# Retention and attention kernel: token sums, decay tables, chunk ends and a gate modulation in other places

## Chip, core and metric

The kernel runs on one core of a Trainium2 chip. The metric is the device time of one execution in microseconds (us). The engines are TensorE (PE, with its weight loads as PEld), VectorE (DVE), ScalarE (ACT), GpSimd (POOL) and SyncE (SP, which here only issues DMAs). DMAs are issued from the queues of SP, ACT and POOL.

## What is computed

Two layers over 256 latent tokens and 256 context tokens of width 2048, batch 1, all in float32. Each layer normalises its input, modulates it by a shift and a scale that come from a condition vector `c` (adaLN), runs a token mixer, multiplies the mixer's result by a SiLU gate of the input, projects it, and adds it back under a gate `gt` that also comes from `c`.

```python
for i in range(DEPTH):                                  # 2 layers
    mod_l = c_act @ ada_w[i] + ada_b[i]                 # shift, scale, gate: 3 x 2048 each
    mod_c = cc_act @ ada_w[i] + ada_b[i]
    sh_l, sc_l, gt_l = jnp.split(mod_l, 3, axis=-1)
    ...
    h_l = _rms_norm(x, norm_gain[i]) * (1 + sc_l[:, None]) + sh_l[:, None]
    h_c = _rms_norm(ctx, norm_gain[i]) * (1 + sc_c) + sh_c
    y_l, y_c = mixer(h_l, h_c, ...)   # layer 0: retention, 8 heads; layer 1: windowed attention, 16 heads
    x = x + gt_l[:, None] * y_l
    if i < DEPTH - 1:
        ctx = ctx + gt_c * y_c
```

The retention mixer scores queries against keys with powers of a decay per head and direction; its scores are multiplied by tables of such powers. The second layer's context result is not needed, so of its gate only the latent tokens' half is computed: the part (1, 2) of the modulation.

## The kernel before

**Products.** Weights stream through SBUF in tiles `wraw` of 512 KB (five buffers, loaded on SP's queue). A float32 product is made of three matmuls, so each tile is split: ACT casts its high half `wh` (L143), DVE subtracts to get the low half `wl` (L114); each has three buffers. TensorE then runs high × high, low × high and high × low (L151 to L153) into PSUM: five accumulators `acc` and three smaller `pm`. A chunk of 512 output columns needs eight such weight tiles.

**Layer 0.** First come the query-key chunks of the first heads, then the value projection of all heads, then a loop over eight heads. In heads 0 to 3 the loop runs one chunk of eight tiles, the head's gate; in heads 4 to 7 a query-key chunk and then the gate chunk. Behind every weight tile a `hook` is called, and it puts in a piece of other work: the previous head's outputs in five tasks (`o0`, `o1`, `norm`, `l0`, `l1`), this head's decay tables (`dc`), scores (`sc`), the values' load and split (`v`, `vs`), and a number of modulation steps. Which task stands behind which tile is written out in lists (`plan`, `begin`). A scheduler then orders each engine's instructions.

**Clearing a chunk.** `evac` rotates the four accumulators of a query-key chunk (rope) and splits them: `t` and `sw` (L975 to L977) and `r_h`, `r_l`. The next chunk's matmuls need those accumulators.

**Modulation steps.** The modulation by `c` is not a matmul: a tile of `adaB` (512 KB, SP's queue) is multiplied by a row of `c` (`crow`) and summed in one DVE instruction (L690), with a short read of the sum behind it. There are 224, all in layer 0: two for each of 96 tiles (latent and context tokens), and one for each of 32 tiles of the part (1, 2).

**Token sums.** The output projection of layer 0 is done with seven products in place of eight (as Strassen's), so it needs sums and differences of the two token blocks of the gated heads, `a` to `d`. `parts` makes five of them per head, M1, M3, M4, M6 and M7, on POOL (L1058, tile `ue`, two buffers), and stores each to DRAM `uB_d` on POOL's queue (L1062); `a` and `d` themselves go out on ACT's queue. For the last head M1 and M4 are made on DVE and stay in SBUF. The projection, right behind, loads the sums back and splits them; its result `x` (L1217, L1218) lies in the memory that the last head's sums leave.

**Decay powers.** At the end of the first chunks the decay powers, transposed in `gT`, go to DRAM (`gamT_d`, `pow_d`), and one DMA of 1024 rows of 1020 bytes copies them skewed into `skew_d` (L656). All of these stand on ACT's queue. The heads read their tables `dd` from `skew_d`.

**Layer 1.** K and V projections, then four query chunks (q0 to q3) and four gate chunks (g0 to g3) in turn; behind each weight tile `pump` puts in two pieces of the attention. The last part is the second output projection.

Of the kernel before, what the change touches and what calls it, by code (L numbers as in the profile page):

```python
# [15 lines left out]
ALU = mybir.AluOpType  # L16
# [6 lines left out]
T = 512  # L23
# [29 lines left out]
def backbone(ctx: ExitStack, tc, xT_d, w0_d, wo0_d, w1_d, wo1_d, adaS_d, adaB_d,  # L53
# [340 lines left out]
    with tc.tile_pool(name="pa", bufs=1) as pa:  # L394
# [218 lines left out]
        for u in range(2, 9):  # L613
# [31 lines left out]
            if u == 7:  # L645

                gp = m_tile()
                with after():
                    pe[0] = nc.tensor.transpose(gp[0:64, 0:P], gam.rearrange("p a b -> p (a b)"), ident).ins
                gT = pb.tile([P, P], F32, name="gT", tag="dd")  # L650
                nc.scalar.copy(gT[0:64], gp[0:64, 0:P])
                nc.scalar.dma_start(out=gamT_d.rearrange("d k h t -> (d k h) t"), in_=gT[0:64])
                nc.scalar.dma_start(out=pow_d[:, 0:127], in_=gT[40:48, 1:P])
                nc.scalar.dma_start(out=pow_d[:, 127:128], in_=ones[0:H, 0:1])
                nc.scalar.dma_start(out=pow_d[:, 128:255], in_=gT[0:H, 0:127])
                nc.scalar.dma_start(out=skew_d.rearrange("h (r x) -> h r x", x=255),  # L656
                                    in_=pow_d.unsqueeze(1).to_broadcast([H, P, 255]))
# [18 lines left out]
    def ada_parts(parts, ntk):  # L676
        for layer, kind in parts:
            part = 3 * layer + kind - 2
            asum = const.tile([P, 2, KB, ntk], F32, name="asum", tag=f"asum{ntk}")
            for q in range(2):  # L680
                if q not in rows_at:
                    rows_at.clear()
                    rows_at[q] = [crow(adap[0], f"crow{t}", t, q) for t in range(2)]
                    yield "row"
# [16 lines left out]
    jobs = chain(ada_parts(((0, 2), (1, 0), (1, 1)), 2), ada_parts(((1, 2),), 1))  # L701
# [10 lines left out]
    with tc.tile_pool(name="ph", bufs=1) as ph:  # L712
# [130 lines left out]
        def hook():  # L843
            count[0] += 1
            n = count[0]
            if n > 4:
                with tc.issue_after(last_lo[0]), tc.issue_after(last_hi[0]):
                    next(stats, None)
            if n <= 4 or n % 2:
                ada_step(2 + (n <= 4))  # L850
            next(sums, None)

# [89 lines left out]
    if True:  # L942
# [108 lines left out]
        def parts(h, u, to=None):  # L1051

            a, b, c, d = (u[k][:, :, L * t:L * t + L] for k in range(2) for t in range(2))
            for m, x, y, op in ((M4, a, c, ALU.subtract), (M1, a, d, ALU.add), (M6, a, b, ALU.add),
                                (M7, c, d, ALU.add), (M3, b, d, ALU.subtract)):
                ue = pb.tile([P, 2, L], F32, name="ue", tag="ue", bufs=2)
                now = to is not None and m in (M1, M4)
                (nc.vector if now else nc.gpsimd).tensor_tensor(out=ue, in0=x, in1=y, op=op)  # L1058
                if now:
# [3 lines left out]
            for m, x in ((M2, a), (M5, d)):  # L1063
                nc.scalar.dma_start(out=uB_d[m, h], in_=x)
# [7 lines left out]
        def output_tasks(h, sg, gated=True):  # L1072
# [10 lines left out]
            def last(f):  # L1083
# [4 lines left out]
                if f and gated:  # L1088
                    parts(h, sg)
# [19 lines left out]
        def begin(plan, ada):  # L1109
            state["plan"], state["ada"] = iter(plan), iter(ada)  # L1110
# [18 lines left out]
        for h in range(H):  # L1129
# [3 lines left out]
            if h < 4:  # L1133
                e = [lambda g=qkr, i=i, h=h: evac(h, g, (i, 2 + i)) for i in range(2)]
                if h:
                    o0, o1, norm, l0, l1 = outs
                    plan = [[o0], [o1, dc], [e[0], v], [e[1], norm], [sc[0]], [l0, sc[1]], [l1, vs, sc[2]], [sc[3]]]
# [4 lines left out]
                begin(plan, [2 * (h > 0 or n > 3) for n in range(8)])  # L1142
            else:
                o0, o1, norm, l0, l1 = outs
                begin([[o0], [o1], [dc], [norm, v], [], [l0], [l1, vs], []], [3, 3, 3, 3, 3, 3, 2, 1])
                accs = gemm_ws(w0_d, 3 * h, 8, h_mov, T, hook=hook)
# [3 lines left out]
                begin([[], [], [], [sc[0]], [sc[1]], [sc[2]], [sc[3]], []], [2] * 8)  # L1150
# [5 lines left out]
        assert not list(jobs)  # L1156
# [3 lines left out]
                outs[1:2] + [(M4, 0), (M4, 1)], outs[2:3] + [(M4, 5), (M4, 6), (M4, 2), (M4, 3)],  # L1160
# [12 lines left out]
        parts(H - 1, sg, {m: unit(m, H - 1) for m in (M1, M4)})  # L1173
# [238 lines left out]
    open_slots("r2z")  # L1412

    with tc.tile_pool(name="pe", bufs=1, side="right") as pe:
# [54 lines left out]
        accs = gemm_ts(w1_d, 1, 8, h1_stat, 4)  # L1469
# [3 lines left out]
        def gate(c):  # L1473
            accs = gemm_ws2(w1_d, 2 + c, 8, 0, hook=lambda: pump(PUMP))
# [6 lines left out]
        def queries(c):  # L1481
            accs = gemm_ts(w1_d, 6 + c, 8, h1_stat, 2, hook=lambda: pump(PUMP))
# [84 lines left out]

        for g in range(4):
            accs = gemm_ws2(wo1_d, g, 8, 1, pre=(lambda kp: pump(5 if kp < 6 else 100)) if g == 0 else None,
                            tail=1 if g < 3 else 2)  # L1570
            for j in range(4):
# [18 lines left out]
                nc.scalar.dma_start(out=out_d[kb], in_=xb)  # L1590
    close_top()
# [102 lines left out]
```

## Time and profile before

| | before |
|---|---|
| median of three runs, us | 1962.4 |
| lowest and highest, us | 1961.68, 1967.97 |
| profiled execution, us | 1965.91 |
| its span, first to last instruction, us | 1964.1 |
| mean granted TensorE clock | 0.995 |
| moved by DMA | 472.95 MB, mean 241 GB/s |

How to read the quoted lines: a line of a timeline gives the start in us, the duration in us, the engine (with q for its queue of DMA issues), the line of the kernel, the operation, output <- input, how many, and in brackets the idle time before it and what ended that. A line of the waits gives engine, what waited, `<-` what ended the wait, the total in us, how many times, the longest. A line of a tile gives min/median/max of one instruction in ns, and the first and last start. A line of the windows gives the stretch, its length, then for PE, PEld, DVE, ACT and POOL the busy us and (x count), the granted clock, the DMA engines' share and GB/s.

### The profile page before, as it was taken

How to read it: one execution, taken by the hardware profiler on the slowest of the kernel's cores; microseconds unless marked ns; L12 is line 12 of the kernel's file. 1: busy time of each engine (PE TensorE's matmuls, PEld its weight loads, DVE VectorE, ACT ScalarE, POOL GpSimd, SP SyncE). 2: the span in 40 equal slices, each digit the busy share in tenths (PEclk: the TensorE clock that was granted, in tenths of full speed). 3: DMA queues.
4: the chain of work that ended last, by engine and by line, in shares of the span. 5: the costliest groups of instructions: out<-in, count | busy, mean ns of one | idle time of the engine just before them, and what ended most of it. 6: DMA issues, size and time to landing. Idle time of an engine off the chain costs nothing.

```text
span 1964.1 us, 26030 instructions
## 1 busy us (share of the span) xinstructions
PE 1917.0 (98%) x9420; PEld 1578.6 (80%) x9420; DVE 1493.0 (76%) x2250; ACT 817.8 (42%) x1218; POOL 401.0 (20%) x446
## 2 busy tenths in 40 slices
PE   8999999999999999999999999899999999999999
PEld 4677878788787788878788778788888888888887
DVE  5577877877868998888888776677879746777764
ACT  4233434334444333222322235355555434766653
POOL 1201222222211444423323231200000000000000
PEclk9999999999999999999999999999999999999999
DMA  9969989989897877888989985579976325444464
GB/s 392 416 251 284 281 243 274 279 269 292 261 288 215 257 225 220 269 249 250 275 258 291 327 265 194 189 257 303 316 261 218 104 95 161 143 137 139 130 204 149
DMA packets 138842, 472.95 MB, mean 241 GB/s; under 512 B 17528, under 2 KB 33368, under 8 KB 133080
## 3 DMA queue, kind: packets, MB, share of 16 engines
q1 hardware_dynamic: 105792, 367.40, 54.3%
q0 software_dynamic: 15200, 49.30, 12.7%
q10 hardware_dynamic: 17720, 54.59, 7.9%
q8 instruction: 74, 1.21, 0.3%
q14 instruction: 56, 0.46, 0.1%
HBM read 440.22 MB, written 99.14 MB: 275 GB/s over the span
## 4 chain that ended last, share of the span: by engine, by line
PE 73%; DVE 12%; DMA 9%; issue 3%; ACT 2%; POOL 1%; ACTq 0%; SPq 0%; DVEq 0%; POOLq 0%
PE acc L153 11%; PE acc L151 11%; PE acc L152 11%; PE acc L1212 9%; PE acc L202 6%; DMA wraw<-in_w 5%; PE acc L1209 4%; DVE wl L114 4%; PE pm L152 3%; PE pm L153 3%; PE pm L151 3%; PE acc L199 3%; PE acc L531 2%; DVE wraw L690 2%; DMA wraw<-in_adaB 2%
## 5 line engine op out<-in xcount | busy, mean ns | idle before, releaser
L114 DVE TENSOR_TENSOR wl<-wraw,wh 128x1024 fp32r<-128x1024 f32 x416 | 510.7, 1234 | 264.6 <-ACT wh L143 256.2
L143 ACT CAST wh<-wraw 128x1024 fp32r<-128x1024 f32 x415 | 433.8, 1051 | 636.4 <-DMA wraw<-in_w 258.2
L151 PE MATMUL acc<-hT_h,wh 128*128 128x512 f32 x928 | 365.4, 394 | 13.0 <-DVE t L975 7.6
L153 PE MATMUL acc<-hT_h,wl 128*128 128x512 f32 x928 | 362.7, 391 | 1.1 <-DVE wl L114 1.1
L152 PE MATMUL acc<-hl,wh 128*128 128x512 f32 x928 | 362.9, 391 | 0.0
L333 POOL COPY pin_t<-wl 128x1 f32<-128x1 f32 x128 | 95.2, 744 | 675.9 <-DVE wl L114 666.9
L151 PEld LDWEIGHTS acc<-hT_h,wh 128*128 128x128 f32 x928 | 175.0, 189 | 53.5 <-issue 10.8
L153 PEld LDWEIGHTS acc<-hT_h,wl 128*128 128x128 f32 x928 | 175.0, 189 | 39.0 <-DVE wl L114 2.0
L152 PEld LDWEIGHTS acc<-hl,wh 128*128 128x128 f32 x928 | 175.2, 189 | 34.7
L690 DVE SCALAR_TENSOR_TENSOR wraw<-wraw,crow 128x1024 f32<-128x1024 f32 x128 | 170.9, 1340 | 6.6 <-DMA wraw<-in_adaB 5.8
L690 DVE SCALAR_TENSOR_TENSOR ajunk<-wraw,crow 128x1024 bf16<-128x1024 f32 x96 | 121.9, 1270 | 6.7 <-DMA wraw<-in_adaB 6.6
L153 PE MATMUL acc<-wh,hl 128*128 128x512 f32 x320 | 125.0, 391 | 0.0
L252 POOL TENSOR_TENSOR rs<-ms,mhalf 128x4 f32<-128x4 f32 (+1 forms) x23 | 28.4, 1236 | 418.2 <-DVE ms L246 306.9
L335 POOL DMA_DIRECT2D wS_d<-in_wo x128 | 101.0, 789 | 11.1 <-issue 8.8
L143 ACT CAST wh<-vt 128x1024 fp32r<-128x1024 f32 x48 | 50.4, 1051 | 99.0 <-DVE vt L117 75.9
L1058 POOL TENSOR_TENSOR ue<-sg 128x512 f32<-128x512 f32 x38 | 71.7, 1893 | 92.7 <-DVE sg L1048 46.5
L114 DVE TENSOR_TENSOR wl<-vt,wh 128x1024 fp32r<-128x1024 f32 x48 | 58.8, 1225 | 38.2 <-ACT wh L143 37.6
L152 PE MATMUL pm<-r_l,r_h 128*128 128x512 f32 (+1 forms) x216 | 75.1, 348 | 5.3 <-DVE r_l L114 5.3
L151 PE MATMUL pm<-r_h 128*128 128x512 f32 (+1 forms) x216 | 75.4, 349 | 3.1 <-DVE sg L1040 2.0
L152 PE MATMUL acc<-wl,hT_h 128*128 128x512 f32 x192 | 75.2, 392 | 0.5 <-DVE wl L114 0.5
L151 PE MATMUL acc<-wh,hl 128*128 128x512 f32 x192 | 75.4, 393 | 0.0
L152 PE MATMUL acc<-wl,hl 128*128 128x512 f32 x192 | 74.9, 390 | 0.0
(315 smaller groups left out, 3695.4 us busy)
## 6 DMA issues: line engine op xcount, KB each, us to landing
wraw<-in_w SPq DMA_DIRECT2D x288, 512.0 KB, 4.9
wraw<-in_adaB SPq DMA_DIRECT2D x128, 512.0 KB, 5.2
wraw<-in_wo SPq DMA_DIRECT2D x80, 512.0 KB, 4.6
wS_d<-in_wo ACTq DMA_DIRECT2D x128, 256.0 KB, 5.3
wS_d<-in_wo POOLq DMA_DIRECT2D x128, 256.0 KB, 6.7
wraw<-wS_d SPq DMA_DIRECT2D x64, 512.0 KB, 5.3
araw<-in_adaS SPq DMA_DIRECT2D x28, 1024.0 KB, 13.1
wraw<-uB_d SPq DMA_DIRECT2D x20, 512.0 KB, 5.5
```

The costliest lines, as they stand in the source:

```text
L114: return nc.vector.tensor_tensor(out=out, in0=a, in1=hi.bitcast(F32), op=ALU.subtract)
L143: last_hi[0] = nc.scalar.copy(wh, raw).ins
L151: nc.tensor.matmul(ps, lhsT=ah, rhs=bh, start=start, stop=False, skip_group_check=skip)
L152: nc.tensor.matmul(ps, lhsT=ah, rhs=bl, start=False, stop=False, skip_group_check=skip)
L153: return nc.tensor.matmul(ps, lhsT=al, rhs=bh, start=False, stop=stop, skip_group_check=skip).ins
L202: nc.tensor.matmul(accs[j], lhsT=wk, rhs=h1(kb, s).rearrange("p a t -> p (a t)"), start=(kb == 0), stop=False)
L333: pin = nc.gpsimd.tensor_copy(pin_t, last_wl[0][:, 0, 0:1].bitcast(F32)).ins
L335: nc.gpsimd.dma_start(out=wS_d[i, r, q, x], in_=wo0_d[(*SUMS[i][1], r, q, x)], accum_op=ALU.add, max_dma_last_dim=4096)
L690: nc.vector.scalar_tensor_tensor(out=junk, in0=flat, scalar=1.0, in1=rows_at[q][t], op0=ALU.mult, op1=ALU.mult, accum_out=asum[:, q, kb, t ...
L1058: (nc.vector if now else nc.gpsimd).tensor_tensor(out=ue, in0=x, in1=y, op=op)
L1209: last_pe[0] = nc.tensor.matmul(accs[j][:, 0:L], lhsT=wk, rhs=b[:, 0:L], start=False, stop=(kq == 3 and k == 3)).ins
L1212: nc.tensor.matmul(accs[j], lhsT=wk, rhs=b, start=(kq == 0 and k == 0), stop=False)
```

## The change

Four parts, which the diff below shows cut to its core.

1. The 32 modulation steps of part (1, 2) leave layer 0 and come in layer 1: one behind each weight tile of the value chunk (`hook1(True)`), then one behind every second tile of the query and gate chunks. Two more loads of `crow` go with them. The numbers of steps per tile in layer 0 are written anew: 4 fewer in each of heads 0 to 3 and in each of heads 4 to 6, 6 fewer in head 7.
2. All token sums are made on DVE. M6 comes with task `l0`, the others with `l1`; M7 and M3 are made in place in the gated head's own tile `sg` and stored from there, M6, M4 and M1 in `ue`. The stores stay on POOL's queue. The tasks of heads 1 to 3 move by up to a tile.
3. Query-key chunks of heads 4 to 7 run their last two weight tiles block by block (`tail=2`): each accumulator takes both tiles before the next begins. The hook that this would skip is called.
4. `gT` and the decay powers are stored on POOL's queue, and the skewed copy is cut into one DMA per head.

```diff
@@ gemm_ws
             elif kp < nkp - 1:
+                if hook is not None:
+                    hook()
                 continue
...
@@ decay powers
-                nc.scalar.dma_start(out=gamT_d.rearrange("d k h t -> (d k h) t"), in_=gT[0:64])
...
-                nc.scalar.dma_start(out=skew_d.rearrange("h (r x) -> h r x", x=255),
-                                    in_=pow_d.unsqueeze(1).to_broadcast([H, P, 255]))
+                nc.gpsimd.dma_start(out=gamT_d.rearrange("d k h t -> (d k h) t"), in_=gT[0:64])
...
@@ hook of the first chunks
+            if n % 2 == 0:
+                i = n // 2 - 1
+                nc.gpsimd.dma_start(out=skew_d[i].rearrange("(r x) -> r x", x=255),
+                                    in_=pow_d[i].unsqueeze(0).to_broadcast([P, 255]))
...
-    jobs = chain(ada_parts(((0, 2), (1, 0), (1, 1)), 2), ada_parts(((1, 2),), 1))
+    jobs = ada_parts(((0, 2), (1, 0), (1, 1)), 2)
...
+        def parts(h, u, k, to=None):
+            a, b, c, d = (u[k2][:, :, L * t:L * t + L] for k2 in range(2) for t in range(2))
+            def made(m, x, y, op):
+                ue = pb.tile([P, 2, L], F32, name="ue", tag="ue", bufs=2)
+                comb(ue, x, y, op)
+                if to is not None and m in to:
+                    split(to[m][:, :, 0:L], to[m][:, :, L:T], ue)
+                else:
+                    nc.gpsimd.dma_start(out=uB_d[m, h], in_=ue)
+            if k == 0:
+                made(M6, a, b, ALU.add)
+                nc.scalar.dma_start(out=uB_d[M2, h], in_=a)
+                return
+            made(M4, a, c, ALU.subtract)
+            made(M1, a, d, ALU.add)
+            for m, x, op in ((M7, c, ALU.add), (M3, b, ALU.subtract)):
+                comb(x, x, d, op)
+                nc.gpsimd.dma_start(out=uB_d[m, h], in_=x)
+            nc.scalar.dma_start(out=uB_d[M5, h], in_=d)
...
@@ heads 1 to 3, then heads 4 to 7
-                    plan = [[o0], [o1, dc], [e[0], v], [e[1], norm], [sc[0]], [l0, sc[1]], [l1, vs, sc[2]], [sc[3]]]
+                    plan = [[o0], [o1, dc, e[0]], [e[1]], [norm, v], [sc[0]], [l0, sc[1]], [vs, sc[2]], [l1, sc[3]]]
...
-                begin([[o0], [o1], [dc], [norm, v], [], [l0], [l1, vs], []], [3, 3, 3, 3, 3, 3, 2, 1])
-                accs = gemm_ws(w0_d, 3 * h, 8, h_mov, T, hook=hook)
+                begin([[o0], [o1], [dc], [norm, v], [], [l0], [l1, vs], []], (4, 4, 1, 2, 2, 1, 1, 0))
+                accs = gemm_ws(w0_d, 3 * h, 8, h_mov, T, hook=hook, tail=2)
...
@@ layer 1
+    jobs = ada_parts(((1, 2),), 1)
+    n1 = [0]
+    def hook1(always=False):
+        pump(PUMP)
+        n1[0] += 1
+        if always or n1[0] % 2:
+            with tc.issue_after(last_lo[0]):
+                next(jobs, None)
...
-        accs = gemm_ts(w1_d, 1, 8, h1_stat, 4)
+        accs = gemm_ts(w1_d, 1, 8, h1_stat, 4, hook=lambda: hook1(True))
...
-            accs = gemm_ws2(w1_d, 2 + c, 8, 0, hook=lambda: pump(PUMP))
+            accs = gemm_ws2(w1_d, 2 + c, 8, 0, hook=hook1)
```

(`comb` is a tensor-tensor operation on DVE, L117, and was there before.) Three places show how instructions move.

The first is ACT's queue behind the first query-key chunk, where the accumulators are copied to `qk0e` and stored to `qk_d`. Before:

```order
L642 COPY qk0e<-acc 128x512 [waits PE_49]
L656 DMA skew_d<-pow_d 1024x1x255 [waits DMAHW4_49,DMAHW2_49]
L643 DMA qk_d<-qk0e 128x512 [waits Activation_49]
L642 COPY qk0e<-acc 128x512 [waits PE_49]
L642 COPY qk0e<-acc 128x512 [waits DVE_49,PE_49]
L643 DMA qk_d<-qk0e 128x512 [waits DMAHW3_49,Activation_49]
```

and POOL's queue at that point of the program after the change (`qk1e` is the second chunk, `pin_t` and `wS_d` belong to the copying of weights for the output projection):

```order
L654 DMA gamT_d<-gT 64x128 [waits Activation_49]
L655 DMA pow_d<-gT 8x127
L657 DMA pow_d<-gT 8x127
L854 DMA skew_d<-pow_d 128x255 [waits DMASW3_49,DMASW2_49,DMASW0_49]
L854 DMA skew_d<-pow_d 128x255 x4
L854 DMA skew_d<-pow_d 128x255 [waits DMASW1_49]
L854 DMA skew_d<-pow_d 128x255 x2
L662 DMA qk_d<-qk1e 128x512 [waits DMASW4_49,DVE_49]
L662 DMA qk_d<-qk1e 128x512 [waits DMASW5_49,DVE_49]
L335 COPY pin_t<-wl 128x1 [waits DVE_49]
```

The skewed copy has left ACT's queue; its eight pieces stand together on POOL's, ahead of the second chunk's stores, although the program issues them in eight different hooks.

The second place is DVE at the end of head 4's query-key chunk (`acc` its accumulators; `wl` low halves of weight tiles, before those of the next chunk's first two tiles, after that of the chunk's own last). Before:

```order
L1048 SCALAR_TENSOR_TENSOR sg<-sg,vec,pm 128x512 x4
L114 TENSOR_TENSOR wl<-wraw,wh 128x1024 x2
L114 TENSOR_TENSOR r_l<-acc,r_h 128x256 x2
L975 TENSOR_TENSOR t_6729<-acc,ropeR 128x256
L976 TENSOR_TENSOR sw<-sw,ropeR 128x256
L975 TENSOR_TENSOR t_6740<-acc,ropeR 128x256
L977 TENSOR_TENSOR t_6729<-t_6729,sw 128x256
L976 TENSOR_TENSOR sw<-sw,ropeR 128x256
L114 TENSOR_TENSOR r_l<-acc,r_h 128x256
```

After:

```order
L114 TENSOR_TENSOR wl<-wraw,wh 128x1024
L1052 SCALAR_TENSOR_TENSOR sg<-sg,vec,pm 128x512 x3
L117 TENSOR_TENSOR ue<-sg 128x512
L1052 SCALAR_TENSOR_TENSOR sg<-sg,vec,pm 128x512
L114 TENSOR_TENSOR r_l<-acc,r_h 128x256
L117 TENSOR_TENSOR ue<-sg 128x512
L117 TENSOR_TENSOR sg<-sg 128x2x256 x2
L117 TENSOR_TENSOR ue<-sg 128x512
L979 TENSOR_TENSOR t_6683<-acc,ropeR 128x256
L980 TENSOR_TENSOR sw<-sw,ropeR 128x256
```

The five sums now stand on DVE between the last weight tile's low half and the clearing of the first accumulator; the steps of clearing come one accumulator at a time.

The third place is DVE at the end of head 7 and the start of the output projection (`z` the last gate, `bop` the split of M1, `x` the projection's first results). Before:

```order
L1172 TENSOR_TENSOR sg<-sg,z 128x512 x2
L114 TENSOR_TENSOR wl<-wraw,wh 128x1024
L1058 TENSOR_TENSOR ue<-sg 128x512 x2
L114 TENSOR_TENSOR wl<-wraw,wh 128x1024
L114 TENSOR_TENSOR r_l<-ue,r_l 128x2x256
L114 TENSOR_TENSOR bop<-ue,bop 128x2x256
L114 TENSOR_TENSOR wl<-wraw,wh 128x1024 x2
```

After:

```order
L1185 TENSOR_TENSOR sg<-sg,z 128x512 x2
L117 TENSOR_TENSOR ue<-sg 128x512 x2
L117 TENSOR_TENSOR sg<-sg 128x2x256 x2
L114 TENSOR_TENSOR wl<-wraw,wh 128x1024
L114 TENSOR_TENSOR r_l<-ue,r_l 128x2x256
L117 TENSOR_TENSOR ue<-sg 128x512
L114 TENSOR_TENSOR wl<-wraw,wh 128x1024
L114 TENSOR_TENSOR bop<-ue,bop 128x2x256
```

Four of the five sums come in one piece before the next low half, and M1 behind it; the three that POOL made after DVE's two are now among them.

More of the change, by code (lines that the diff above doesn't have):

```diff
@@ L682, in ada_parts @@
                     rows_at.clear()
-                    rows_at[q] = [crow(adap[0], f"crow{t}", t, q) for t in range(2)]
+                    rows_at[q] = [crow(adap[0], f"crow{t}", t, q) for t in range(ntk)]
                     yield "row"
@@ L1154, in backbone @@
                 nc.scalar.activation(sg[j // 2][:, j % 2, :], accs[j], AF.Silu)
-        assert not list(jobs)
+        left = list(jobs)
+        assert not left, len(left)
         sg = gates(H - 1)
@@ L1566, in backbone @@
                     attend(c, t)
+        left = list(jobs)
+        assert not left, len(left)
         for g in range(4):
@@ L1590, in backbone @@
                 nc.scalar.dma_start(out=out_d[kb], in_=xb)
+    adap_cm.__exit__(None, None, None)
     close_top()
```

35 lines of the change are left out of this document (15 added, 20 removed).

## The prediction

> **What bounds the kernel now.** I read the page's busy times first, then the chain that ended last, then TensorE's waits, then the windows by stage.
>
> ```profile
> PE 1917.0 (98%) x9420; PEld 1578.6 (80%) x9420; DVE 1493.0 (76%) x2250; ACT 817.8 (42%) x1218; POOL 401.0 (20%) x446
> ...
> PE 73%; DVE 12%; DMA 9%; issue 3%; ACT 2%; POOL 1%; ACTq 0%; SPq 0%; DVEq 0%; POOLq 0%
> ```
>
> TensorE (PE) is busy for 1917.0 of 1964.1 us. The change takes no matmul away, so all it can win is in the 47 us when PE stands still, plus matmuls that ran at a lower clock after such a stop. The list of PE's waits says what those are (total, times, longest); what is not in these six rows the change leaves alone, as the start of the kernel.
>
> ```profile
> PE acc L151 <- DVE t L975: 7.6, 5, 3.2
> PE pm L1212 <- ACT wh L143: 5.3, 1, 5.3
> PE pm L152 <- DVE r_l L114: 5.3, 4, 1.9
> ...
> PE acc L151 <- ACT wh L143: 3.7, 4, 2.7
> ...
> PE pm L151 <- DVE sg L1040: 2.0, 1, 2.0
> PE pm L260 <- POOL ossq L1044: 1.2, 1, 1.2
> ```
>
> The first row is the clearing of a query-key chunk's accumulators, the second the start of the first output projection, the third the split of a head's operands, the fourth mostly one stop at 160 us, the last two lie in head 7. Four stretches of granted clock 0.50 follow such stops (columns: stretch and length, then PE, PEld, DVE, ACT, POOL busy, and the clock):
>
> ```profile
> 845.80:849.20 3.40, 3.40 (x9) 2.61 (x8) 2.91 (x6) 1.56 (x4) 2.75 (x4) 0.50 0.78 176
> 1245.20:1252.00 6.80, 4.99 (x14) 3.86 (x15) 5.94 (x9) 4.97 (x8) 0.00 (x0) 0.50 0.37 99
> 671.75:675.20 3.45, 3.02 (x8) 2.53 (x9) 3.45 (x9) 1.06 (x1) 1.85 (x3) 0.51 1.12 321
> 1132.55:1136.00 3.45, 3.45 (x10) 2.71 (x9) 2.04 (x2) 0.83 (x1) 0.00 (x0) 0.51 0.91 284
> ```
>
> At half clock half of the PE time is lost: 1.7, 2.5, 1.5 and 1.7 us. A stop that goes should take its stretch along.
>
> **Decay powers off ACT's queue.** Before, the wide table copy stands on ACT's queue among the q/k stores, and a cast behind it comes late:
>
> ```profile
> 140.91 0.78 ACTq L656 DMA_DIRECT2D skew_d<-pow_d  x1
> ...
> 142.19 7.44 ACTq L643 DMA_DIRECT2D qk_d<-qk0e  x1
> ...
> 159.38 1.04 ACT L143 CAST wh<-wraw 128x1024 fp32r<-128x1024 f32 x1 [6.27 <-DMA skew_d<-pow_d]
> ```
> ```profile
> 160.48 0.50 PE L151 MATMUL acc<-hT_h,wh 128*128 128x512 f32 x1 [2.67 <-ACT wh L143]
> ```
>
> The store took 7.44 us to issue, the cast waited 6.27 us, PE 2.67 us for the cast and a little more for the low half that DVE makes of it; I let the whole be 3.5 at most. After the change only the four q/k stores stand there. The eight table copies move to POOL's queue, all ahead of four other q/k stores and of the weight-pinning pairs; the tables' first reader is far off:
>
> ```profile
> L990 POOL DMA_DIRECT2D dd<-skew_d x8: 539/574/590, 563.8 to 1096.7; - x8
> ```
>
> Bounds: 0 (the stores are slow by themselves) to −3.5; I take **−3**, as the wait names the table copy. The Trainium skill (DMA: Bandwidth & Descriptors, "Issuing engines are not separate DMA queues") says that another issuing engine gives no bandwidth, only the issuer's time, as all share 16 DMA engines. If the transfers themselves were the limit here, the term would be 0 and the forecast 1946; the row shows ACT's own queue held, so I keep the term.
>
> **Sums of token blocks.** 36 sums go from POOL to DVE.
>
> ```profile
> L1058 POOL TENSOR_TENSOR ue<-sg x38: 1252/1466/9622, 654.8 to 1241.5; 128x512 f32<-128x512 f32 x38
> ...
> L1058 DVE TENSOR_TENSOR ue<-sg x2: 682/682/683, 1224.1 to 1224.7; 128x512 f32<-128x512 f32 x2
> ...
> DMA to landing us min/median/max: 2.3/3.8/6.9
> ```
>
> On DVE they are about 36 × 0.68 = 24.5 us. But DVE already pays while POOL adds:
>
> ```profile
> L976 DVE TENSOR_TENSOR sw<-sw,ropeR x32: 408/418/2410, 567.7 to 1167.2; 128x256 f32<-128x256 f32 x32
> ```
> ```profile
> 844.83 2.41 DVE L976 TENSOR_TENSOR sw<-sw,ropeR 128x256 f32<-128x256 f32 x1
> ```
> ```profile
> 845.36 1.58 POOL L1058 TENSOR_TENSOR ue<-sg 128x512 f32<-128x512 f32 x1
> ```
> ```profile
> 845.05 0.47 PE L151 MATMUL acc<-hT_h,wh 128*128 128x512 f32 x1 [3.20 <-DVE t L975]
> ```
>
> A 0.42 us step of clearing a chunk took 2.41 us with a sum on POOL at its end, and PE waited 3.20 us just there. So the exchange is about even in DVE time, and it removes a delay at the worst place. The Trainium skill (SBUF — State Buffer, "Who interferes with whom") states that a DVE instruction with two SBUF inputs contends with a GpSimd instruction that reads SBUF, one blocking the other. The trace agrees (2.41 against 0.42 us); without that rule the sums would cost DVE 24 us more and the forecast would be some 4 us later (heads 0 to 3 at 0).
>
> **Query-key chunks block by block (heads 4 to 7).** With the last two weight tiles combined, each of the four accumulators takes 4 × 3 matmuls, and they start 0.227 us apart (rows below: 1155.14 to 1155.82 is three), so it ends 2.7 us after the one before; the first ends 8.2 us before the chunk, not 4.1. Clearing one takes five steps of at most 0.42 us, 2.1 us, so three are done before the end. The row of 7.6 us and its clock stretch (1.7) can go: −9.3; the near bound is that only the longest stop (3.2) goes, with the collision: −3. I take **−8**, since the list of waits has nothing else at these places. The price: the last tile's low half is needed 8.2 − 4.1 = 4.1 us sooner. The tightest is head 7:
>
> ```profile
> 1150.64 1.22 DVE L114 TENSOR_TENSOR wl<-wraw,wh 128x1024 fp32r<-128x1024 f32 x1
> ```
> ```profile
> 1155.14 0.39 PE L151 MATMUL acc<-hT_h,wh 128*128 128x512 f32 x1
> 1155.37 0.39 PE L152 MATMUL acc<-hl,wh 128*128 128x512 f32 x1
> 1155.60 0.39 PE L153 MATMUL acc<-hT_h,wl 128*128 128x512 f32 x1
> 1155.82 0.39 PE L151 MATMUL acc<-hT_h,wh 128*128 128x512 f32 x1
> ```
>
> Made at 1151.9 and used at 1155.6, a lead of 3.7 us: 0.4 us short, inside the 8. The sum M1 now waits on DVE until M6's store has left their common buffer: 0.6 us to issue and 3.8 to land, against some 3.1 us of DVE work between, so about 1.3 us. Behind it is the clearing of the first accumulator, which is due some 8 us later; no cost.
>
> **End of head 7.**
>
> ```profile
> 1227.18 9.62 POOL L1058 TENSOR_TENSOR ue<-sg 128x512 f32<-128x512 f32 x1 [19.63 <-DVE r_l L114]
> ...
> 1243.06 0.56 POOL L1062 DMA_DIRECT2D uB_d<-ue  x1 [0.30 <-POOL ue L1058]
> ```
> ```profile
> 1245.64 0.38 ACT L1217 ACTIVATE x<-acc 128x256 f32<-128x256 f32 x1 [11.14 <-DMA uB_d<-ue]
> ```
> ```profile
> 1247.01 4.00 PE L1212 MATMUL pm<-r_l,wh 128*128 128x512 f32 x8 [5.33 <-ACT wh L143]
> ```
>
> One POOL sum takes 9.62 us behind a busy DVE, two more follow, the last store is issued at 1243.06, and ACT's `x`, whose memory it holds, starts at 1245.64; the cast behind that lets PE go at 1247.01. After: three more sums of 0.68 us on DVE behind the two that it makes already (1224.1, 1224.7), with a weight split between, so done by about 1230; 0.6 us to issue and 2.0 to land (as 1243.06 to 1245.64) give 1233. PE asks at 1247.01 − 5.33 = 1241.7, and the cast is then long made. This gives 5.3 + 2.5 = 7.8; the sums put 1.4 us ahead of a weight split and SyncE's queue waits some 2 us for the stores (a row of `crow` in it needs that memory), so the near bound is −5. I take **−7.5**.
>
> **Heads 0 to 3 and 7.** Four modulation steps fewer in each of heads 0 to 3:
>
> ```profile
> L690 DVE SCALAR_TENSOR_TENSOR wraw<-wraw,crow x128: 1207/1220/2721, 141.3 to 1143.1; 128x1024 f32<-128x1024 f32 x128
> L690 DVE DVE_READ_ACCUMULATOR wraw<-wraw,crow x128: 74/81/88, 142.5 to 1144.3; 128x1 f32 x128
> ```
> ```profile
> 610.00:720.00 110.00, 106.06 (x501) 88.48 (x500) 100.75 (x170) 40.26 (x72) 39.92 (x34) 0.98 0.75 228
> 720.00:850.00 130.00, 124.55 (x582) 103.69 (x581) 114.14 (x171) 40.12 (x66) 63.17 (x63) 0.99 0.80 244
> ```
>
> Each step is 1.22 + 0.08 = 1.30 us, so 5.2 us fewer in each, where DVE (third busy number) is at 92% and 88%. The `r_l` waits (5.3) and their clock stretch (1.5) could go, −6.8; the new order of steps and sums could also delay others, +3. I take **−3**. Head 7's two rows and their stretch are 4.9 us together; six steps fewer there help, but neither engine's cause is removed: 0 to −5, I take **−1.5**.
>
> **Layer 1.** The 32 steps come back, 42 us of DVE and 32 loads.
>
> ```profile
> 1578.00:1631.00 53.00, 52.98 (x241) 43.15 (x240) 26.53 (x37) 18.20 (x26) 4.77 (x4) 1.00 0.28 90
> ...
> 1730.00:1780.00 50.00, 50.00 (x263) 42.28 (x262) 38.11 (x67) 34.54 (x60) 2.63 (x2) 1.00 0.45 147
> ```
> ```profile
> L1477 ACT COPY sgT<-acc x16: 345/372/395, 1676.2 to 1860.0; 128x256 f32<-128x256 f32 x16
> ```
>
> Seven go into the value chunk (first window): 26.5 + 9 of 53 us of DVE, no danger. The other 25 stand one per two weight tiles. The row of `sgT` marks the ends of the first gate chunk and of the last, six chunks of eight tiles later: 183.8 / 48 = 3.8 us a tile, so a step in 7.7 us, 1.30 / 7.7 = 17% of DVE. That lifts the second window from 76 to 93%. PE waits nowhere there now (50.00 of 50). In 610 to 720, at 92%, PE lost 3.9 of 110 us, part of it to POOL's sums; over the 190 us of these chunks that rate is 6.8, and I let it be up to 12, as DVE is in the attention's chain. Bounds 0 to +12, I take **+4**. The loads meet a DMA share of 0.28 to 0.45, so they hide.
>
> **Sum:** −3 −8 −7.5 −3 −1.5 +4 = −19 on the profiled execution's 1965.9 (span 1964.1 and 1.8 around it) gives 1946.9. That execution is 3.5 us above the runs' median of 1962.4; from the median, 1943.4.
>
> **Rivals.** (1) *New waits in the heads:* the sums and the earlier splits cost as much as the collisions did, so only the decay powers, the end of head 7 and 3 us of the chunks' clearing stay: −3 −7.5 −3 +4 = −9.5, 1953. For it: 88 to 92% on DVE; against: the 2.41 us row. (2) *All off the path:* every bound at its good end, −3.5 −9.3 −7.8 −6.8 −4.9 +0 = −32, 1930. For it: each of these stops has one named cause that the change touches; against: DVE at 93% in layer 1. (3) *Layer 1 the bound, the other side:* each step stands ahead of a weight's low half or of the attention's short steps on DVE, and PE waits for it. The gains of 23 are used up once 18 of the 32 steps (23 / 1.30) reach PE in full; all 32 give 1962.4 − 23 + 42 = 1981. Against it: 7% of DVE still free at the fullest place. (4) *It doesn't do what it says:* the table copies block POOL's queue instead, M1's wait holds DVE at the end of each head, and layer 1 takes 12: near 0, 1961.
>
> **How the numbers follow.** A measurement here tells some 0.3%, 6 us, from no change: 1956.5 and 1968.3. Chances: forecast 0.54, rival 1 0.20, rival 2 0.10, rival 3 0.08, rival 4 0.08. Faster is the forecast, rival 2 and three quarters of rival 1 (the rest slips above 1956.5): 0.79; same is rival 4 and that rest: 0.13; slower 0.08. The range runs from rival 2, with two us for short waits left out here, 1928, up to 1960, short of rivals 3 and 4.
>
> **What would show it.** Right: no row of PE waiting for `t` at a chunk's end; no POOL sum among the groups; ACT's `x` no longer behind a store of sums; the cast at 159 us without a wait; no clock stretch at 0.50 behind these. Wrong: PE waiting for `wl` at the last two tiles of a query-key chunk, DVE idle before `ue` for a store, or PE below 99% of the layer-1 windows.

## The result, and the profile after

| | before | after |
|---|---|---|
| median, us | 1963.53 (4 runs, 1961.68 to 1967.97) | 1932.07 (4 runs, 1930.9 to 1933.82) |
| ratio to before, 95% interval | | 0.9837 [0.9818, 0.9856] |
| span of the profiled execution, us | 1964.1 | 1932.0 |
| mean granted clock | 0.995 | 0.998 |

The change takes 31.5 us off, 1.6%. The forecast was 1943, 19 us below the median that was known then, in a range of 1928 to 1960: the direction and the range hold, and the gain is 1.6 times the forecast one. Rival 2, "all off the path", had 1930. (One execution of the run no_tail below took 6670.42 us at a granted clock of 0.333; that run's median is of its other three.)

The page's busy times and the chain that ended last, after the change:

```profile
PE 1908.9 (99%) x9420; PEld 1576.7 (82%) x9420; DVE 1480.2 (77%) x2288; ACT 823.6 (43%) x1220; POOL 335.0 (17%) x420
...
PE 77%; DVE 5%; DMA 3%; ACT 1%; issue 1%; POOL 0%; ACTq 0%; SPq 0%; DVEq 0%; POOLq 0%
```

PE stood still for 47.1 us before (1964.1 − 1917.0) and for 23.1 after (1932.0 − 1908.9). That is 24 of the 32 us; the other 8 are PE's own busy time, which fell by 8.1 us with the same 9420 matmuls, as the stretches at half clock went. PE's waits, after (total, times, longest):

```profile
PE pm L425 <- DMA x<-in_xT: 5.1, 1, 5.1
PE acc L533 <- ACT hT_h L287: 3.0, 2, 1.8
PE pm L152 <- DVE wl L114: 2.5, 6, 0.8
PE acc L151 <- ACT sg L1166: 2.1, 1, 2.1
PE acc L152 <- DVE wl L114: 1.6, 2, 0.9
PE acc L151 <- ACT stash L861: 1.0, 1, 1.0
```

Of the six rows of the prediction `t` (7.6), `r_l` (5.3) and `sg` (2.0) are gone, the 5.3 us at the output projection too, and the other two have 0.5 us each; what leads now is the kernel's start. One stop is new: PE waits 2.1 us for ACT's `sg` at head 0, and the granted clock is 0.50 behind it, from 606 to 608 us; in the run after_again below this wait is 0.4 us. The windows, after:

```profile
610.00:720.00 110.00, 109.45 (x525) 91.60 (x524) 93.86 (x171) 43.46 (x77) 29.99 (x34) 1.00 0.72 222
720.00:850.00 130.00, 130.00 (x616) 109.04 (x615) 100.40 (x171) 40.79 (x65) 37.07 (x44) 1.00 0.75 228
...
1600.00:1700.00 100.00, 100.00 (x517) 84.87 (x516) 87.65 (x146) 59.94 (x95) 4.64 (x4) 1.00 0.71 232
1700.00:1800.00 100.00, 99.14 (x504) 82.77 (x503) 84.27 (x153) 67.49 (x114) 3.33 (x3) 1.00 0.60 194
```

In these 240 us of the heads PE is busy for 239.45 us, where it was for 230.6. In layer 1 DVE went up to 84 to 88% and PE lost 0.9 us.

To see where the time went, the trace is cut at three points of the program: the first SiLU of head 0's gate, the first matmul of the output projection, and the first one behind it. Before:

```profile
601.58 0.59 ACT L1154 ACTIVATE sg<-acc 128x512 f32<-128x512 f32 x1
```
```profile
1216.28 0.94 PE L1212 MATMUL acc<-r_h,wh 128*128 128x512 f32 x3
...
1538.78 0.40 PE L151 MATMUL acc<-wh,hl 128*128 128x512 f32 x1
```

After:

```profile
600.33 0.59 ACT L1166 ACTIVATE sg<-acc 128x512 f32<-128x512 f32 x1
```
```profile
1191.97 1.40 PE L1226 MATMUL acc<-r_h,wh 128*128 128x512 f32 x5
...
1506.47 0.40 PE L151 MATMUL acc<-wh,hl 128*128 128x512 f32 x1
```

So the heads took 614.7 and take 591.6 us, the output projection 322.5 and 314.5, and all behind it 425.3 and 425.5 (the span less the third point). The start took 601.6 and takes 600.3; between executions of one kernel it varies more than that, see the runs below.

### The profile page after: what moved, and what is told of

It reads as the page before. It is cut to its first block, busy times and chain, and to the rows that moved or that the text cites. A ratio compares the mean times of both kernels' runs of the same rounds, so it can differ in the third digit from the quotient of the medians.

```text
span 1932.0 us, 26074 instructions
## 1 busy us (share of the span) xinstructions
PE 1908.9 (99%) x9420; PEld 1576.7 (82%) x9420; DVE 1480.2 (77%) x2288; ACT 823.6 (43%) x1220; POOL 335.0 (17%) x420
## 4 chain that ended last, share of the span: by engine, by line
PE 77%; DVE 5%; DMA 3%; ACT 1%; issue 1%; POOL 0%; ACTq 0%; SPq 0%; DVEq 0%; POOLq 0%
PE acc L152 13%; PE acc L151 13%; PE acc L153 13%; PE acc L1226 9%; PE acc L204 6%; PE acc L1223 5%; PE pm L152 4%; PE pm L153 4%; PE pm L151 4%; PE acc L201 3%; DVE wl L114 2%; PE pm L1226 2%; DMA wraw<-in_w 1%; ACT wh L143 1%; PE pm L1223 1%; DVE vt L117 1%
## 5 line engine op out<-in xcount | busy, mean ns | idle before, releaser
L335 POOL COPY pin_t<-wl 128x1 f32<-128x1 f32 x128 | 90.0, 703 | 708.7 <-DVE wl L114 693.5
L690 DVE SCALAR_TENSOR_TENSOR wraw<-wraw,crow 128x1024 f32<-128x1024 f32 x128 | 159.5, 1246 | 0.3
L254 POOL TENSOR_TENSOR rs<-ms,mhalf 128x4 f32<-128x4 f32 (+1 forms) x23 | 32.5, 1411 | 413.1 <-DVE ms L248 302.1
L151 PE MATMUL acc<-wh,hT_h 128*128 128x512 f32 x192 | 74.0, 392 | 0.6 <-ACT wh L143 0.5
```

Of the source, the lines that this page charges most:

```text
L151: nc.tensor.matmul(ps, lhsT=ah, rhs=bh, start=start, stop=False, skip_group_check=skip)
L335: pin = nc.gpsimd.tensor_copy(pin_t, last_wl[0][:, 0, 0:1].bitcast(F32)).ins
L690: nc.vector.scalar_tensor_tensor(out=junk, in0=flat, scalar=1.0, in1=rows_at[q][t], op0=ALU.mult, op1=ALU.mult, accum_out=asum[:, q, kb, t ...
```

## The experiments

The kernels ran in three groups, each group on one chip, and all ratios are to the kernel before, run beside them. The stages are those above (to 0.2 us), from the profiled execution of each.

| run | median, us | ratio, 95% interval | start | heads | output proj. | rest |
|---|---|---|---|---|---|---|
| before (in the three groups) | 1966.02, 1967.18, 1964.73 | 1 | 601.6 | 614.7 | 322.5 | 425.3 |
| only_sums | 1971.86 | 1.0032 [1.0017, 1.0046] | 604.7 | 628.7 | 314.6 | 425.4 |
| only_tail | 1963.39 | 0.9991 [0.9973, 1.0009] | 599.0 | 614.5 | 321.5 | 425.4 |
| only_layer1 | 1947.90 | 0.9917 [0.989, 0.9943] | 599.0 | 598.2 | 322.3 | 426.0 |
| only_decay | 1960.38 | 0.9981 [0.9964, 0.9998] | 598.9 | 614.1 | 322.7 | 424.9 |
| no_sums | 1935.73 | 0.9843 [0.9814, 0.9873] | 595.8 | 593.6 | 318.4 | 425.8 |
| no_tail | 1932.62 | 0.9825 [0.9791, 0.986] | 593.8 | 596.2 | 314.4 | 425.7 |
| no_layer1 | 1947.02 | 0.9903 [0.9872, 0.9933] | 595.9 | 609.5 | 314.4 | 424.9 |
| no_decay | 1933.85 | 0.9833 [0.9798, 0.9868] | 599.7 | 591.5 | 314.4 | 425.9 |
| after_again | 1928.09 | 0.9814 [0.9799, 0.9828] | 594.9 | 591.1 | 314.4 | 425.7 |
| steps_only | 1935.36 | 0.9849 [0.9826, 0.9872] | 599.7 | 597.8 | 314.4 | 424.7 |
| loads_only | 1949.48 | 0.9921 [0.9905, 0.9938] | 598.6 | 610.1 | 314.4 | 424.8 |
| double_l1 | 1939.39 | 0.9869 [0.9854, 0.9884] | 594.1 | 590.9 | 314.4 | 434.3 |

The changed kernel itself has 1932.07 on one chip and 1928.09 on another, with starts of 600.3 and 594.9. So 4 us between groups say nothing; within a group, and in the stages, less can be read.

### One part alone, on the kernel before

**only_sums**: all sums on DVE, through the two `ue` buffers, nothing in place.

```diff
-                (nc.vector if now else nc.gpsimd).tensor_tensor(out=ue, in0=x, in1=y, op=op)
+                nc.vector.tensor_tensor(out=ue, in0=x, in1=y, op=op)
```

> The kernel before with one edit: all token sums on DVE (no in-place, no other order). Theory A (POOL's sums stop DVE, and that makes most stops in the heads): the end of head 7 gives -8 and the heads -12 or more, so about 1943; PE's waits for t and r_l of the split shrink to less than a third. Theory B (the terms as predicted: only the end of head 7 gains by the sums, the heads about nothing): about 1955. Theory C (DVE's load in the heads counts, and 36 x 0.68 = 24.5 us more of it hurts): 1958 or more.

It is slower than before, by 0.3%. Theories A and B were wrong. Theory C's "1958 or more" holds, but the load that it named, the additions' own 0.68 us each, is only a part of it: the output projection gains its 8 us, and the heads lose 14. DVE's waits, PE's waits, and DVE at the end of head 7's query-key chunk in this run:

```profile
DVE ue L1058 <- DMA uB_d<-ue: 20.9, 11, 5.1
```
```profile
PE acc L151 <- DVE t L975: 14.2, 6, 5.0
```
```profile
1172.09 1.32 DVE L1058 TENSOR_TENSOR ue<-sg 128x512 f32<-128x512 f32 x2 [1.10 <-DMA uB_d<-ue]
1173.33 0.42 DVE L975 TENSOR_TENSOR t<-acc,ropeR 128x256 f32<-128x256 f32 x1
```

Five sums through two buffers make DVE wait for the stores, 20.9 us in all, and the clearing (`t`) stands behind. What POOL could wait for at no cost, DVE can't. How much of the 14 us is this wait and how much the time of the additions, no run tells.

**only_tail**: the block-by-block end alone (with the hook that it would skip, as in the change).

```diff
-                accs = gemm_ws(w0_d, 3 * h, 8, h_mov, T, hook=hook)
+                accs = gemm_ws(w0_d, 3 * h, 8, h_mov, T, hook=hook, tail=2)
```

> The kernel before with one edit: the last two weight tiles of the query-key chunks of heads 4 to 7 block by block. Theory A: POOL's sums still collide with the clearing, at most half of the stops (7.6 us and a clock stretch of 1.7) goes: about 1959. Theory B: the early start hides the collision too, -8: about 1955. Theory C: the last low half is needed 4.1 us sooner on a full DVE, so gains are given back: 1963.

No change that can be measured, as theory C had it. The waits for `t` do fall, but the heads take 614.5 us as before. PE's waits in this run have a larger row for `wl`, which was 1.1 us before. It takes back 2.6 of the 5.8 us; where the rest went isn't shown.

```profile
PE acc L153 <- DVE wl L114: 3.7, 5, 1.3
...
PE acc L151 <- DVE t L977: 1.8, 1, 1.8
```

**only_layer1**: the 32 steps in layer 1 alone, with the new numbers of steps per tile.

```diff
-    jobs = chain(ada_parts(((0, 2), (1, 0), (1, 1)), 2), ada_parts(((1, 2),), 1))
+    jobs = ada_parts(((0, 2), (1, 0), (1, 1)), 2)
...
+    jobs = ada_parts(((1, 2),), 1)
```

> The kernel before with one edit: the 32 modulation steps of part (1, 2) in layer 1, with the new numbers of steps per tile in layer 0. Theory A: heads lose only the stops that DVE's load makes, -3, layer 1 costs 0 to 2: about 1962. Theory B: -4.5 in the heads, +4 in layer 1: about 1963. Theory C: 42 us less on DVE in layer 0 is the main gain, -15: about 1949.

Theory C, by its size: 0.83% faster, 16.5 us in the heads. The wait for `t` falls from 7.6 to 1.8 us without any other order of the clearing. Whether it is DVE's 42 us, as C had it, or the loads that left with the steps, this run doesn't tell.

**only_decay**: the decay powers on POOL's queue alone.

```diff
-                nc.scalar.dma_start(out=skew_d.rearrange("h (r x) -> h r x", x=255),
-                                    in_=pow_d.unsqueeze(1).to_broadcast([H, P, 255]))
+                nc.gpsimd.dma_start(out=skew_d[i].rearrange("(r x) -> r x", x=255),
+                                    in_=pow_d[i].unsqueeze(0).to_broadcast([P, 255]))
```

> The kernel before with one edit: decay powers stored and skewed on POOL's queue. All theories: -2 to -3, about 1961, with PE's stop at 160 us gone. If the stores to DRAM are slow by themselves: no change, 1963.5, and the cast still waits.

0.19% faster, 3.7 us by the ratio: as expected, though the interval reaches nearly to no change. PE's stop at 160 us is gone from its waits. The start is 2.7 us shorter than before in the profile, but so it is in only_tail and only_layer1, which still have that stop (2.9 and 2.0 us), so the length of the start shows nothing.

Alone, the four give +0.32 −0.09 −0.83 −0.19 = −0.79%; together they give −1.63%. They need each other.

### One part taken back, from the changed kernel

**no_sums** (the sums that go to DRAM on POOL, two of them in place), **no_tail** (`tail=2` taken back), **no_layer1** (the 32 steps back in layer 0 with the old numbers of steps per tile), **no_decay** (decay powers and skewed copy on ACT's queue):

```diff
-                comb(x, x, d, op)
+                nc.gpsimd.tensor_tensor(out=x, in0=x, in1=d, op=op)
```
```diff
-                accs = gemm_ws(w0_d, 3 * h, 8, h_mov, T, hook=hook, tail=2)
+                accs = gemm_ws(w0_d, 3 * h, 8, h_mov, T, hook=hook)
```
```diff
-    jobs = ada_parts(((0, 2), (1, 0), (1, 1)), 2)
+    jobs = chain(ada_parts(((0, 2), (1, 0), (1, 1)), 2), ada_parts(((1, 2),), 1))
```
```diff
-                nc.gpsimd.dma_start(out=gamT_d.rearrange("d k h t -> (d k h) t"), in_=gT[0:64])
+                nc.scalar.dma_start(out=gamT_d.rearrange("d k h t -> (d k h) t"), in_=gT[0:64])
...
+                nc.scalar.dma_start(out=skew_d.rearrange("h (r x) -> h r x", x=255),
+                                    in_=pow_d.unsqueeze(1).to_broadcast([H, P, 255]))
```

> The changed kernel with the sums that go to DRAM on POOL again, the in-place ones too; order, tail, steps and decay powers as changed. Theory D (the parts need each other: the steps out of layer 0 and the early chunk ends make room on DVE for the sums, which then give the end of head 7): +8 at the end of head 7 and 0 to +3 in the heads by collisions, about 1942. Theory E (each part is worth what it was alone, the sums +6): 1926.

> The changed kernel without the block-by-block end of the query-key chunks of heads 4 to 7. Theory D: the sums stand on DVE ahead of the clearing of the accumulators again, PE waits for t as in the run with the sums alone (14.2 us there, less with fewer steps): +6 to +10, about 1940. Theory E: +2, 1934.

> The changed kernel with the 32 modulation steps of part (1, 2) back in layer 0, with the old numbers of steps per tile. Theory D: +16 for the steps and some more, since the sums now stand on a full DVE, -1 in layer 1: 1950 to 1957. Theory E: +16, 1948.

> The changed kernel with the decay powers and the skewed copy on ACT's queue again. Both theories: +2 to +4, about 1935, with PE's stop at 160 us back.

Only no_layer1 differs clearly in the ratio, and by the stages it loses 18 us in the heads (609.5 against 591.6). Its 1947 is what E had, and below D's range: the sums add nothing that can be seen to what the steps cost by themselves. no_sums speaks for D: it is not faster without DVE's sums, as E had it; its heads are 2 us longer and its output projection 4, half of the 8 that D had there. no_tail is 4.6 us longer in the heads, nearer to D, while its median shows nothing against the changed kernel on another chip; and the stop isn't where D had put it. PE doesn't wait for `t`, but at 890, 992 and 1096 us, early in the next head's query-key chunk, for the step of DVE that multiplies the previous head's outputs by its gate. How this hangs on the early end isn't shown.

```profile
PE pm L151 <- DVE sg L1044: 3.9, 3, 2.4
```

no_decay shows no difference in the ratio either, but has PE's stop at 160 us back (2.4 us), by the same cast:

```profile
160.98 1.04 ACT L143 CAST wh<-wraw 128x1024 fp32r<-128x1024 f32 x1 [5.54 <-DMA skew_d<-pow_d]
```

### What of the 32 steps counts: DVE's time or the loads

Two kernels split no_layer1. **steps_only** has the 32 steps in layer 0 at full size, without their loads; **loads_only** has the loads, and the step works on 16 of 1024 columns. Neither computes the second layer's gate, and both have the old numbers of steps per tile, as no_layer1 has. **after_again** is the changed kernel beside them, and **double_l1** adds a second step of the same size behind each in layer 1.

```diff
-                    raw = load_raw(adaB_d[16 * part + kb, q].rearrange("p (a c) -> p a c", a=2))
+                    if ntk == 2:
+                        raw = load_raw(adaB_d[16 * part + kb, q].rearrange("p (a c) -> p a c", a=2))
...
-                        flat = raw.rearrange("p a c -> p (a c)")
+                        flat = raw.rearrange("p a c -> p (a c)") if ntk == 2 else rows_at[q][0]
```
```diff
+                        m = slice(0, 16 if ntk == 1 else 1024)
                         nc.vector.scalar_tensor_tensor(
-                            out=junk, in0=flat, scalar=1.0, in1=rows_at[q][t],
+                            out=junk[:, m], in0=flat[:, m], scalar=1.0, in1=rows_at[q][t][:, m],
```
```diff
+                        if ntk == 1:
+                            a2 = const.tile([P, 1], F32, name="asum2", tag="asum2")
+                            nc.vector.scalar_tensor_tensor(
+                                out=flat, in0=flat, scalar=1.0, in1=rows_at[q][t],
+                                op0=ALU.mult, op1=ALU.mult, accum_out=a2)
```

> The changed kernel once more, on the chip of the three runs beside it, as their measure: ratio 0.984 to the kernel before.

> The run with the 32 steps back in layer 0, without their 32 loads: each step multiplies the resident crow by itself, so the second layer's gate is not computed. Theory F (DVE's time is what the heads lack): as with the loads, +13 to +16 against the changed kernel. Theory G (the loads take weight buffers and SP's queue, and weights come late): +0 to +4.

> The run with the 32 steps back in layer 0, with their loads, but each step works on 16 of 1024 columns, so the second layer's gate is not computed. Theory F: +0 to +4 against the changed kernel. Theory G: +10 to +16.

> The changed kernel with each of the 32 steps in layer 1 followed by a second one of the same size, whose sum is thrown away: 40 us more on DVE there. If DVE in layer 1 is near its limit, as the prediction's +4 to +12 had it: 10 to 25 us longer, with PE waiting for wl and for the attention's steps in 1630 to 1800. If it has room, since these steps fit into its idle time: less than 4.

Against 1928.09 beside them, steps_only is 7.3 us longer and loads_only 21.4. Neither theory has both numbers (F: 13 to 16 and 0 to 4; G: 0 to 4 and 10 to 16); the loads have the larger part, as G had it. In the heads it is 6.7 and 19.0 us; with both, in no_layer1, 18. So the two do not add up: the loads alone cost as much as both. The wait of ACT's casts for weights, in the runs before, no_layer1, loads_only, steps_only and after_again in this order:

```profile
ACT wh L143 <- DMA wraw<-in_w: 258.2, 60, 8.8
```
```profile
ACT wh L143 <- DMA wraw<-in_w: 250.9, 61, 9.2
```
```profile
ACT wh L143 <- DMA wraw<-in_w: 253.9, 61, 10.5
```
```profile
ACT wh L143 <- DMA wraw<-in_w: 197.4, 51, 10.6
```
```profile
ACT wh L143 <- DMA wraw<-in_w: 194.5, 47, 10.0
```

(Total, times, longest.) In these five it is 251 to 258 us where the 32 loads are in layer 0 and 195 to 197 where they aren't, whether the steps are there or not; over all runs here, 226 (only_tail) to 265 (only_decay) with them and 178 (no_sums) to 210 (no_tail) without. So weights come later with the loads. But that is not what PE mostly stops for. This row of loads_only is absent from after_again:

```profile
PE acc L153 <- DVE wl L114: 11.8, 6, 3.3
```

The longest of its six stops lies at the end of head 7's query-key chunk. The last tile's cast, the store of M6, the sum M1, that tile's low half, and PE:

```profile
1137.45 1.05 ACT L143 CAST wh<-wraw 128x1024 fp32r<-128x1024 f32 x1 [2.62 <-DMA wraw<-in_w]
```
```profile
1140.04 0.60 POOL L1066 DMA_DIRECT2D uB_d<-ue  x1 [1.48 <-DVE ue L117]
```
```profile
1147.09 0.69 DVE L117 TENSOR_TENSOR ue<-sg 128x512 f32<-128x512 f32 x1 [4.56 <-DMA uB_d<-ue]
...
1149.03 1.22 DVE L114 TENSOR_TENSOR wl<-wraw,wh 128x1024 fp32r<-128x1024 f32 x1
```
```profile
1150.31 0.79 PE L153 MATMUL acc<-hT_h,wl 128*128 128x512 f32 x1 [3.27 <-DVE wl L114]
```

The cast waited 2.62 us for its weights, but it was done at 1138.5, over 10 us before DVE began the low half. DVE was held by M1, which takes the buffer of M6 and so waits for M6's store. Four of the six stops, 10.0 of the 11.8 us, stand like this behind M1 (at 828, 932, 1037 and 1150 us), and so do all three of steps_only in its row (5.6 us). In after_again M1 comes 2.4 us after that store is issued, without a wait:

```profile
1120.81 0.60 POOL L1065 DMA_DIRECT2D uB_d<-ue  x1 [5.31 <-DVE ue L117]
```
```profile
1123.22 0.69 DVE L117 TENSOR_TENSOR ue<-sg 128x512 f32<-128x512 f32 x1
```

From the issue of M6's store to M1 it is 4.6 to 7.1 us in the four chunks of loads_only and at most 2.8 in those of after_again. Of all that PE waits in the heads, the stops behind M1 are 10.0 of 15.0 us in loads_only, 5.6 of 6.7 in steps_only, and 4.4 of 12.8 in no_layer1, where late casts, the gating step `sg` and POOL's `ossq` have some 2 each. So put back one at a time, loads and steps stop PE mostly through this store, and only little through late weights. Why the store takes longer is open: in steps_only it takes 5.0 to 6.3 us in three of the four chunks without the 32 loads, and no run has the steps back in layer 0 with other numbers of steps per tile near the chunk's end.

double_l1 is 11.3 us longer, 8.6 of them behind the output projection, about as the first of its two cases had it. The windows of layer 1, after_again and then double_l1, and PE's wait in double_l1:

```profile
1600.00:1700.00 100.00, 100.00 (x524) 85.08 (x523) 88.81 (x155) 61.66 (x102) 4.64 (x4) 1.00 0.70 232
```
```profile
1600.00:1700.00 100.00, 97.36 (x502) 80.86 (x500) 96.16 (x171) 58.31 (x97) 4.33 (x4) 1.00 0.64 210
```
```profile
PE acc L201 <- DVE wl L114: 4.6, 3, 2.3
```

At 89% DVE still keeps up there, at 96% not: the first 42 us of steps cost 1 us at most, the next 40 some 9.

## Why the prediction was right, and where its sizes were off

**Direction.** Right: all six rows that it named went or fell to 0.5 us, and the four clock stretches with them. What made them go is in part not what it named, as the next paragraphs say. Two slips of its working weigh little: the sums that move are 38, as its own row shows (x38), and not 36, so 25.9 us of DVE in place of 24.5; and with heads 0 to 3 at 0 the forecast would be 3 us later, not 4.

**End of head 7** (−7.5): right, in size and mechanism. The output projection is 8 us shorter in each run with DVE's sums, only_sums among them. In no_sums it is still 4 us shorter than before, with POOL adding two of its sums in place; which part of the change keeps these 4 us was not run. POOL and ACT there, after the change:

```profile
1200.83 1.39 POOL L1075 DMA_DIRECT2D uB_d<-sg  x2 [0.61 <-DVE sg L117]
```
```profile
1210.68 0.38 ACT L1231 ACTIVATE x<-acc 128x256 f32<-128x256 f32 x1
```

The last store of a sum is issued about 9 us ahead of ACT's `x`, where it was 2.6 us ahead before.

**Decay powers** (−3): the stop went as named; about −2.5 by the stops, which the ratios of only_decay and no_decay are too coarse to confirm. The stop of 3.5 us is gone, but a smaller one (`stash`, 1.0 us) comes at 195 us instead. The skewed copies did hold POOL's queue until 152 us, and no wait of PE names it:

```profile
152.38 0.57 POOL L662 DMA_DIRECT2D qk_d<-qk1e  x1 [3.92 <-DMA skew_d<-pow_d]
```

**Heads: this is where the size was off.** The three terms there were −8 for the chunks, −3 for heads 0 to 3 and −1.5 for head 7, −12.5 in all; measured is −23. The step that was mis-sized is "Each step is 1.22 + 0.08 = 1.30 us, so 5.2 us fewer in each": it priced the moved steps as DVE time in heads 0 to 3, allowed a little in head 7, and put the 12 steps that leave heads 4 to 6 at nothing. The moved steps alone, in only_layer1, gave 16.5 us, and nearly all of it behind head 3. Cut also at the first SiLU of the gates of heads 3 and 6, before, only_layer1 and after:

```profile
780.46 0.59 ACT L1154 ACTIVATE sg<-acc 128x512 f32<-128x512 f32 x1
...
1097.05 0.59 ACT L1154 ACTIVATE sg<-acc 128x512 f32<-128x512 f32 x1
```
```profile
776.42 0.59 ACT L1154 ACTIVATE sg<-acc 128x512 f32<-128x512 f32 x1
...
1085.00 0.59 ACT L1154 ACTIVATE sg<-acc 128x512 f32<-128x512 f32 x1
```
```profile
773.46 0.60 ACT L1166 ACTIVATE sg<-acc 128x512 f32<-128x512 f32 x1 [1.23 <-PE acc L153]
...
1079.32 0.59 ACT L1166 ACTIVATE sg<-acc 128x512 f32<-128x512 f32 x1
```

| part of the heads, us | before | only_layer1 | after |
|---|---|---|---|
| to head 3's gate | 178.9 | 177.4 | 173.1 |
| from there to head 6's gate | 316.6 | 308.6 | 305.9 |
| from there to the output projection | 119.2 | 112.2 | 112.7 |

So the moved steps by themselves are worth 1.5, 8.0 and 7.0 us in the three parts, and 16 to 18 of the heads' 23 us hang on them and their loads (only_layer1, no_layer1). Put back, they cost nothing before head 3's gate (169.2 us to it in no_layer1, 172.5 in after_again). On the kernel before, no run parts the loads from DVE's time. On the changed kernel the loads weigh more (19 against 7 us in the heads, put back one at a time), there mostly through the sums' stores, as shown above.

**The chunks' ends** (−8): the stops did go, but not by the mechanism that the term names. The block-by-block end alone gave nothing in the heads; the moved steps alone took the wait for `t` from 7.6 to 1.8. In the changed kernel the early end is worth some 5 us in the heads (no_tail). That it gives room for the sums, which now stand ahead of the clearing, is argued and not shown: the stops of no_tail lie elsewhere.

**The sums** ("about even in DVE time"): right only for the form that the change has. Alone and through two buffers they cost 14 us in the heads, where DVE waits for stores. In the changed kernel, with two made in place, DVE's wait for a store is 0.4 us in all, where the prediction had 1.3 a head and called it no cost. But the two in place don't do it alone: with the 32 steps back in layer 0 it is far more, in no_layer1 and then in steps_only, and it did cost:

```profile
DVE ue L117 <- DMA uB_d<-ue: 14.8, 7, 4.1
```
```profile
DVE ue L117 <- DMA uB_d<-ue: 10.3, 5, 3.5
```

The collision with POOL was real, as the longest `sw` shows: 2.41 us before, and after the change, then in no_sums with POOL's sums put back:

```profile
L980 DVE TENSOR_TENSOR sw<-sw,ropeR x32: 410/418/427, 568.3 to 1139.3; 128x256 f32<-128x256 f32 x32
```
```profile
L980 DVE TENSOR_TENSOR sw<-sw,ropeR x32: 413/422/4510, 564.6 to 1139.0; 128x256 f32<-128x256 f32 x32
```

But though one `sw` takes 4.51 us in no_sums, PE has no wait for the clearing there, and the heads lose only 2 us. So a collision need not cost PE anything when the clearing begins early; the stop of 3.2 us at 845 us was not the collision's alone.

**Layer 1** (+4): at most +1. The rate of loss was taken from heads 0 to 3, where DVE was at 92% and PE lost 3.9 of 110 us. DVE's share by itself wasn't the cause there, as no_layer1 shows with the same share, no sums on POOL, and hardly a loss:

```profile
610.00:720.00 110.00, 109.78 (x527) 92.05 (x526) 99.83 (x184) 44.37 (x79) 31.39 (x34) 1.00 0.77 242
```

double_l1 shows that the limit is near, but beyond these steps.

**Rivals.** Rival 2 (all off the path, 1930, given 0.10) came true to 2 us in the number. Its ground, that each stop has one named cause that the change touches, did not: the steps that left heads 4 to 7 were at work in several of them. The heads' 23 us exceed even this rival's 21 there (9.3, 6.8 and 4.9), so that the total came inside the range is in part luck. Rival 1 (sums and early ends cost as much as the collisions) holds for each of the two parts alone, not for the whole.

## What to carry to other kernels

A step that is moved takes its loads with it, and it leaves every stage that it stood in: price it in each of them, and run its time and its loads apart. Where work moves to an engine on the critical path, count the buffers through which its results leave, since this engine will wait for them, and price that wait by the longest landing that the profile shows (6.9 us in the prediction's row, where it took the median of 3.8). And follow a wait back over each engine: a matmul that waits for a low half of weights need not wait for weights.

## What the runs showed of the hardware

Beside GpSimd additions of two SBUF operands (the sums of `sg`), a DVE step of 0.42 us took 2.41 us before and 4.51 us in no_sums, there beside three of them in a row; in the runs without these sums on GpSimd the longest of the 32 equal steps was 0.43 us (only_sums, after). GpSimd's 24 additions for `ossq` stayed in all of them. What keeps a sum's buffer for 4.6 to 7.1 us from the issue of its store, in place of 2.8 or less, the runs leave open. DMA moved a little more with the 32 loads; no_layer1 first, then steps_only, then after_again:

```profile
780.00:1090.00 310.00, 303.84 (x1393) 252.10 (x1392) 263.12 (x440) 90.33 (x143) 83.07 (x100) 0.99 0.87 271
```
```profile
780.00:1090.00 310.00, 304.25 (x1393) 252.63 (x1392) 266.09 (x446) 91.66 (x144) 82.06 (x100) 0.99 0.82 248
```
```profile
780.00:1090.00 310.00, 310.00 (x1438) 258.99 (x1437) 253.66 (x426) 94.34 (x147) 86.08 (x101) 1.00 0.84 256
```

The last two numbers are the DMA engines' share and GB/s: 0.87 and 271, 0.82 and 248, 0.84 and 256. Since steps_only has slow stores at the lowest share, the share of a long window doesn't explain them.
